# Delta rule: values scaled by the key norm in the input projection, written by an identity product into the bank of the error sum, and copied by ScalarE

## The chip, the cores and the metric

The kernel runs on one core of a Trainium2 chip. The metric is the device time of one execution in microseconds (us); lower is better. A profile is one execution recorded by the hardware profiler, whose times count from the start of its span. The engines are named as in the profile: PE is TensorE's matmul, PEld its weight load, DVE is VectorE, ACT is ScalarE, POOL is GpSimd, and SP is the queue from which most transfers (DMAs) are issued. PSUM is the memory that PE writes, in eight banks. Lines of the kernel are written L613.

## The reference, cut to what matters

A two-layer encoder step over 2048 prompt tokens and 32 sample tokens. The first layer is a gated delta rule with 8 heads of 128 channels; the change lies there.

```
proj = x @ w_in                                   # q, k, v rows, then the gate z
qkv  = silu(causal_conv(proj_qkv))                # four taps per channel
q = l2norm(q) / sqrt(128);  k = l2norm(k)
S_t = exp(g_t) (I - beta_t k_t k_t^T) S_{t-1} + beta_t k_t v_t^T
o_t = S_t^T q_t                                   # evaluated exactly, in chunks
```

In a chunk, the error of the values is `v - (k * exp(gcum)) S`: what the new values hold beyond what the state S already predicts. A triangular inverse turns the errors into the changes of the state. The kernel does not normalize k in advance. It works with the raw k, which is the normalized k times its norm, and so needs the values times that norm: `v * hn - (k_raw * exp(gcum)) S`, with hn the key's norm for each token and head.

## The kernel before, in words

**Input projection (up to about 610 us).** `P1.qkv` runs 24 rows, each one head's 128 channels of q (rows 0 to 7), k (8 to 15) or v (16 to 23) over all 2080 tokens. A row is five blocks of 416 tokens, each with 24 matmuls into one PSUM bank (L77 to L79). The banks of these blocks are six: two in pool `ppl`, four in pool `ppr`. ACT copies each block into the row's buffer `R` (L309), of which there are two, so row i + 2 needs the buffer of row i. Then come the four taps (L293 on ACT, three times L295 on DVE) into `y` (two buffers), a tanh on ACT (L275), the product that makes the silu (L276, DVE), and the store of y to DRAM (L278 on SP; a small remainder on ACT's queue). q and k rows also give sums of squares. After row 15 `norms` computes hn (L456) from them, with a power on POOL (L468). Beside this, `presplit` splits weights of later stages (L95, L96) and stores them (L97). Here the order on every engine and queue is chosen by the framework's planner, which simulates a timeline as it places instructions. It is fixed before the run.

**Between the stages (about 610 to 745 us).** The rows' memory is given up (`mid.close()`), and its place is taken by tiles whose loads (L512, L514, L529, L532) SP issues. PE goes on with the gate z, whose blocks are finished by L321 on ACT and L322, L323 on DVE and stored at L324. Two chunks' triangular inverses are computed ahead by DVE.

**Delta loop (`Delta.run`, about 745 to 1165 us).** There are 17 chunks: chunk 0 is the 32 sample tokens, chunks 1 to 16 are 128 prompt tokens each. Iteration i finishes chunk i (`ch`), and prepares chunks i + 1 (`nx`), i + 2 (`n2`) and i + 3 (`n3`). On PE, DVE and ACT the instructions run in exactly the order in which `run` steps through generators (`go`), each step being one `yield`. The names that matter:

- `lower` (L562, L563, L567, L570, L572): products of keys, and the matrix L for the triangular chain.
- `chain` (L585, L588): the triangular inverse, its first 25 of 31 steps on POOL, the rest (t in `run`) on DVE.
- `spread` (L653, L654): transposes of the inverse, tcp; `invert` (L672 to L708): the larger inverse out of the blocks. L672 on PE needs tcp, and L674 on ACT, which writes y1, needs L672.
- `turn_v` (L612, L613): per half of four heads, four transposes of v into a bank of the pair "tr", then one DVE instruction that multiplies by hn into the tile vn.
- `errors` (L717, L718): per half, four products k S into a bank of the pair "sc", then one DVE subtraction from vn.
- `changes` (L728, L730): the inverse times vn; `seen` (L742, L746, L750): the output, two products into one bank, copied by ACT; `squares` (L776) and `powers` (L636) on ACT; `advance` (L760, L766): the new state S; `inside` (L627, L628): q k products gq, into a bank of "tr"; `fade` (L644): k and q times exp(gcum); `emit` (L802, L803): output transposed, times z.
- `fill`: in iterations 0 to 10 it hands PE pieces of the rest of the z projection (L77 to L79, 6 matmuls a piece) at fixed places.

In an iteration the order around the change is: advance, seen, squares of the first half; the second half of seen; squares; `powers(n2)`; a filler; errors, t, spread; turn_v, errors; inside; a filler; invert and the rest.

Of the kernel before, what the change touches and what calls it, by code (L numbers as in the profile page):

```python
# [10 lines left out]
F32 = mybir.dt.float32  # L11
# [3 lines left out]
ALU = mybir.AluOpType  # L15
# [5 lines left out]
NP = 2048  # L21
NS = 32
NT = NP + NS
# [3 lines left out]
H = 8  # L27
# [4 lines left out]
NTT = 17  # L32
# [130 lines left out]
class P1:  # L163
# [49 lines left out]
    def qkv(self):  # L213
        nc, I, T, G, big, one = self.nc, self.I, self.T, self.G, self.big, self.one
# [11 lines left out]
        for b in range(NB):  # L226
            ps = self.ps()
            xh, xl = self.x[b]
            for k in range(KC):
                nc.tensor.matmul(ps[:48, :TB], wab[:, k, :48], xh[:, k, :], start=(k == 0), stop=False,  # L230
                                 skip_group_check=True)
# [3 lines left out]
            for t in range(b * TB // 128, NTT if b == NB - 1 else (b + 1) * TB // 128):  # L235
                n = min(128, NT - t * 128)
# [13 lines left out]
        for i in range(24):  # L250
            kind, h = i // 8, i % 8
            if i < 2:
                R = Rs[i]
            else:
                w = split_weights(nc, self.wp, I["w_in"][i], nc.gpsimd)
                R = self.row(i)
                if i == 23:
                    gate = self.split_gate(nc.gpsimd)
                    first = next(gate)
                for b in range(NB):  # L260
                    self.block(R, w, b)
# [12 lines left out]
            th = one.tile([128, NT + 3], F32, tag="th", name="th")  # L274
            nc.scalar.activation(th[:], y[:], AF.Tanh, scale=0.5)  # L275
            nc.vector.scalar_tensor_tensor(out=y[:], in0=th[:], scalar=1.0, in1=y[:], op0=ALU.add, op1=ALU.mult)  # L276
            dst = T["qkv"[kind]]
            nc.sync.dma_start(dst[0:NTT - 1, :, h, :].rearrange("t p k -> p t k"),  # L278
                              y[:, 0:NP].rearrange("p (t k) -> p t k", k=128))
            nc.scalar.dma_start(dst[NTT - 1, :, h, 0:NS], y[:, NP + 3:NP + 3 + NS])  # L280
            if kind == 2:
                continue
            nc.scalar.activation(th[:, 0:NP], y[:, 0:NP], AF.Square)
            nc.scalar.activation(th[:, NP:NT], y[:, NP + 3:NP + 3 + NS], AF.Square)
            nc.vector.transpose(R[:, 0:NT], th[:, 0:NT])
            nc.vector.tensor_reduce(out=parts[:, h, :], in_=R[:, 0:NT].rearrange("p (c j) -> p c j", j=32),
                                    axis=AX.X, op=ALU.add)
            if h == 7:
                norms(nc, G, parts, self.sel, kind, one, self.pt)
        nc.sync.dma_start(self.O["conv"][:, :, :], self.convo[:])  # L290

    def conv(self, y, R, i, a, z):
        self.nc.scalar.activation(y[:, a:z], R[:, a:z], AF.Copy, scale=self.convw[:, i, 0:1])  # L293
# [146 lines left out]
def norms(nc, G, parts, sel, kind, one, pt):  # L440
    V = nc.vector
    ps = pt.tile([128, 512], F32, tag="tp", name="n_ps")
    pv = ps[:, 0:H * NTT].rearrange("p (h t) -> p h t", h=H)
    for c in range(4):
        m = NTT if c == 0 else NTT - 1
        nc.tensor.matmul(pv[:, :, 0:m], sel[:, c, :], parts[:, :, c::4], start=(c == 0), stop=(c == 3))
    w = H * NTT
    x = one.tile([128, w], F32, tag="n_x", name="n_x")
    V.tensor_scalar(out=x[:].rearrange("p (t h) -> p t h", h=H), in0=pv.rearrange("p h t -> p t h"),
                    scalar1=4e-6, scalar2=None, op0=ALU.add)  # L450
    xv = x[:].rearrange("p (t h) -> p t h", h=H)
    if kind == 0:
        V.tensor_scalar(out=G["eq"][:], in0=xv, scalar1=128.0 * RMS_EPS, scalar2=None, op0=ALU.mult)
        return
    rv = rsqrt_power(nc, G, one, x[:], 128, w, "n")[:].rearrange("p (t h) -> p t h", h=H)
    V.scalar_tensor_tensor(out=G["hn"][:], in0=xv, scalar=0.5, in1=rv, op0=ALU.mult, op1=ALU.mult)  # L456
# [20 lines left out]
class Delta:  # L477
# [124 lines left out]
            ch.kd.append(kd)  # L602
            yield

    def turn_v(self, ch):
        nc, G, n = self.nc, self.G, ch.n
        ch.vn = []
        for q in range(2):
            vn = self.four.tile([128, 4, 128], F32, tag="vn", name="vn")
            tr = self.pa.tile([128, 4, 128], F32, tag="tr", name="vtr")  # L610
            for j in range(4):
                nc.tensor.transpose(tr[:n, j, :], ch.v[q][:, j, :n], G["ident"][:, :])  # L612
            nc.vector.tensor_tensor(out=vn[:n], in0=tr[:n], in1=self.bc(G["hn"][:n, ch.ti, q * 4:q * 4 + 4], n),  # L613
                                    op=ALU.mult)
            ch.vn.append(vn)
            yield

    def inside(self, ch):

        nc, V, n = self.nc, self.nc.vector, ch.n  # L620
# [18 lines left out]
    def fade(self, ch):  # L639

        n = ch.n
        for x in (ch.k, ch.q):
            for q in range(2):
                self.nc.vector.tensor_tensor(out=x[q][:, :, :n], in0=x[q][:, :, :n], in1=ch.gb[q][:, :, :n], op=ALU.mult)  # L644
                yield

    def spread(self, ch):
# [62 lines left out]

    def errors(self, ch):

        nc, V, n = self.nc, self.nc.vector, ch.n
        for q in range(2):
            ks = self.pc.tile([128, 4, 128], F32, tag="sc", name="ks")
            for j in range(4):
                nc.tensor.matmul(ks[:n, j, :], ch.k[q][:, j, :n], self.S[q][:, j, :], start=True, stop=True)  # L717
            V.tensor_tensor(out=ch.vn[q][:n], in0=ch.vn[q][:n], in1=ks[:n], op=ALU.subtract)  # L718
            yield

    def changes(self, ch):
# [85 lines left out]
    def run(self, chunks, S, first, second, side, done):  # L807
# [7 lines left out]
        def go(*gens):  # L815
            for g in gens:
                next(g, None)

        c0, c1, c2 = chunks[:3]
        for c in (c0, c1):  # L820
            for name in ("gb", "k", "q"):
                self.load(c, name)
            if c is c0:
                self.load(c, "v")
# [6 lines left out]
        k, w, g, d, low = self.turn_k(c0), self.turn_v(c0), self.inside(c0), self.decays(c1), self.lower(c1)  # L831
        for s, us in ((w, 0.6), (k, 0.6), (w, 0.6), (k, 0.6), (g, 0.6), (g, 0.6), (d, 0.0), (d, 0.0), (d, 1.2), (d, 1.2),
                      (low, 1.2), (low, 1.2)):
            go(s)
            fill(us)
        drain(self.powers(c0))
        drain(self.fade(c0))
        self.load(c1, "v")
        self.load(c2, "gb")
        self.spread(c0)  # L840
        k, w, g = self.turn_k(c1), self.turn_v(c1), self.inside(c1)
        for s, us in ((k, 1.0), (w, 1.0), (k, 1.0), (w, 1.0), (g, 1.0), (g, 1.0)):
# [6 lines left out]
        go(e, e, seen)  # L849
        self.load(c2, "k")  # L850
        self.load(c2, "q")
        last, z, x = None, none, self.fade(c1)
# [1 line left out]
        for i in range(len(chunks) + 1):  # L854
# [7 lines left out]
                                                   (lambda c: self.chain(c, V, self.SPLIT, 31), nx)))  # L862
            low = gen(self.lower, n2)
            go(low, x, low)
            if n2:
                self.load(n2, "v", (0,))
# [8 lines left out]
            fill(2 * more)  # L875
            go(seen, a, t, a, t)
            fill(more)
            go(sq, seen)
            if n2:
                self.load(n2, "v", (1,))  # L880
            if n3:
                self.load(n3, "q", (0,))
            side()
# [13 lines left out]
            if i == 0:  # L897
                self.save("s_delta")
                self.S = S
            k, w, g, e, v, r, o = (gen(f, c) for f, c in (  # L900
                (self.turn_k, n2), (self.turn_v, n2), (self.inside, n2), (self.errors, nx), (self.invert, nx),
                (self.norms, ch), (self.scale, ch)))
            go(e, t, t)
            drain(t)
            if nx:
                self.spread(nx)
            go(w, e)
            if n3:
                self.load(n3, "k")
            go(g)  # L910
# [1 line left out]
            d = gen(self.decays, n3)  # L912
            go(v, r, r, r, g, r, r, v, r, k, r, d)
            side()
            go(v, w, r, d)
            if i:
                self.load(ch, "z")
            fill(more)
            seen = gen(self.seen, nx)
            go(r, r, seen, v, k, d, r, r)  # L920
            if n3:
# [1 line left out]
            fill(more)  # L923
            drain(r)
            go(o)
            side()
            if i in (13, 14):
                second.step()
# [1091 lines left out]
def host_inputs(inp):  # L2020
# [56 lines left out]
    "v": (NTT, 128, 8, 128),  # L2077
    "z": (8, 128, NT),
    "gcum": (NTT, 8, 128),
    "o": (NS, 8, 128),  # L2080
    "g": (NTT, 128, 8, 128),
    "h": (NT, D),
# [50 lines left out]
```

## Time and profile before

| | |
|---|---|
| time, median of 3 runs | 2183.53 us (2180.78 to 2184.08) |
| the profiled execution's own time | 2181.37 us |
| its span, first to last instruction | 2179.6 us |
| mean granted TensorE clock | 0.986 |
| instructions | 37384 |
| PE busy over the span | 2068.7 us, 95% |
| DVE, ACT, POOL busy | 1477.4, 906.8, 725.1 us |

Busy time is a sum over stages that have different limits, so it is read by stage. A timeline row gives start, length, engine, line, what is written from what, and in brackets how long the engine had stood and for whom. The iterations of the delta loop are told apart by tcp (L653), which runs once in each: iteration 0 at 760.15 us, 2 at 809.27, 6 at 913.53, 9 at 990.04, 13 at 1088.23. An fp32 product on PE shows as two records, a transpose as one.

### The profile page before, as it was taken

How to read it: one execution, taken by the hardware profiler on the slowest of the kernel's cores; microseconds unless marked ns; L12 is line 12 of the kernel's file. 1: busy time of each engine (PE TensorE's matmuls, PEld its weight loads, DVE VectorE, ACT ScalarE, POOL GpSimd, SP SyncE). 2: the span in 40 equal slices, each digit the busy share in tenths (PEclk: the TensorE clock that was granted, in tenths of full speed). 3: DMA queues.
4: the chain of work that ended last, by engine and by line, in shares of the span. 5: the costliest groups of instructions: out<-in, count | busy, mean ns of one | idle time of the engine just before them, and what ended most of it. 6: DMA issues, size and time to landing. Idle time of an engine off the chain costs nothing. (4 is left out here: it accounts for less than half of the span.)

```text
span 2179.6 us, 37384 instructions
## 1 busy us (share of the span) xinstructions
PE 2068.7 (95%) x13494; PEld 1874.1 (86%) x13494; DVE 1477.4 (68%) x2767; ACT 906.8 (42%) x2405; POOL 725.1 (33%) x1194
## 2 busy tenths in 40 slices
PE   8999999999989999999789999999999988999998
PEld 6999999999989889888778887899999976777666
DVE  5788977886557588888875665555645655666663
ACT  5545545444422476767662111411221033444441
POOL 1212211151111187878861220000000053666565
PEclk9999999999999999999999999999999999999999
DMA  7755655557764644534845675988888885433321
GB/s 283 226 187 192 214 180 185 188 180 244 257 211 157 209 128 153 163 130 152 274 144 148 209 264 192 340 290 278 291 279 282 283 291 168 110 85 93 99 81 58
DMA packets 342410, 430.28 MB, mean 197 GB/s; under 512 B 69952, under 2 KB 269984, under 8 KB 342208
## 3 DMA queue, kind: packets, MB, share of 16 engines
q1 hardware_dynamic: 304016, 304.78, 44.0%
q10 hardware_dynamic: 38208, 123.10, 16.9%
q8 instruction: 107, 1.75, 0.3%
q14 instruction: 79, 0.65, 0.1%
HBM read 269.72 MB, written 158.44 MB: 196 GB/s over the span
## 5 line engine op out<-in xcount | busy, mean ns | idle before, releaser
L77 PE MATMUL ps<-act_hi,w_hi 128*128 128x416 f32 x1280 | 458.6, 358 | 5.7 <-DVE z L322 2.5
L79 PE MATMUL ps<-act_hi,w_lo 128*128 128x416 f32 x1280 | 450.5, 353 | 4.7 <-POOL w_lo L54 3.3
L78 PE MATMUL ps<-act_lo,w_hi 128*128 128x416 f32 x1280 | 451.1, 352 | 0.0
L77 PEld LDWEIGHTS ps<-act_hi,w_hi 128*128 128x128 f32 x1280 | 242.0, 189 | 10.1 <-DVE z L322 4.3
L79 PEld LDWEIGHTS ps<-act_hi,w_lo 128*128 128x128 f32 x1280 | 241.9, 189 | 9.5 <-POOL w_lo L54 4.4
L78 PEld LDWEIGHTS ps<-act_lo,w_hi 128*128 128x128 f32 x1280 | 242.6, 190 | 2.8
L1330 PE MATMUL ps<-xs_h,w 128*128 128x416 f32 x560 | 199.6, 356 | 7.8 <-DVE ra L1391 6.6
L1331 PE MATMUL ps<-xs_l,w 128*128 128x416 f32 x560 | 199.9, 357 | 0.5 <-DVE xs_l L1228 0.5
L54 POOL TENSOR_TENSOR w_lo<-w_raw,w_hi 128x1024 fp32r<-128x1024 f32 x32 | 81.5, 2547 | 355.2 <-ACT w_hi L53 341.2
L1332 PE MATMUL ps<-xs_h,w 128*128 128x416 f32 x560 | 198.6, 355 | 0.0
L295 DVE SCALAR_TENSOR_TENSOR y<-R,convw,y 128x2083 f32<-128x2083 f32 (+2 forms) x78 | 175.1, 2245 | 24.5 <-ACT y L293 24.3
L1615 ACT ACTIVATE P<-S,nm 128x192 f32<-128x192 f32 (+2 forms) x260 | 105.3, 428 | 177.4 <-DVE nm L1604 170.8
L585 POOL TENSOR_TENSOR tm<-L,Tt 128x60 f32<-128x60 f32 (+19 forms) x375 | 136.3, 363 | 94.2 <-PE sp L760 48.9
L588 POOL TENSOR_TENSOR Tt<-Tt,tm 128x60 f32<-128x60 f32 (+19 forms) x375 | 142.0, 379 | 28.3
L1530 POOL MEMSET vd<- 64x768 f32 (+2 forms) x10 | 7.8, 776 | 398.1 <-DVE ra L1391 397.8
L1627 POOL TENSOR_TENSOR P<-P,sm 128x512 f32<-128x512 f32 (+2 forms) x126 | 101.7, 831 | 87.8 <-DVE sm L1624 69.2
L1330 PEld LDWEIGHTS ps<-xs_h,w 128*128 128x128 f32 x560 | 106.5, 190 | 10.6 <-DVE ra L1391 7.3
L1391 DVE SCALAR_TENSOR_TENSOR ra<-ps,u 128x416 f32<-128x416 f32 x60 | 35.4, 590 | 117.3 <-PE ps L1332 110.7
L1052 PE MATMUL po<-wo,g_hi 128*128 128x512 f32 (+1 forms) x272 | 110.0, 404 | 0.9 <-DVE hT L1100 0.9
L1332 PEld LDWEIGHTS ps<-xs_h,w 128*128 128x128 f32 x560 | 107.1, 191 | 1.3
L1331 PEld LDWEIGHTS ps<-xs_l,w 128*128 128x128 f32 x560 | 106.3, 190 | 2.1 <-DVE xs_l L1228 0.7
L95 ACT CAST pre_hl<-pre_raw 128x256 fp32r<-128x256 f32 x184 | 65.6, 404 | 101.4 <-DMA pre_raw<-in_b_w_z 25.8
(313 smaller groups left out, 4723.6 us busy)
## 6 DMA issues: line engine op xcount, KB each, us to landing
w<-s_w ACTq DMA_DIRECT2D x180, 512.0 KB, 4.5
s_w<-pre_hl SPq DMA_DIRECT2D x160, 256.0 KB, 2.5
w_raw<-in_w_in SPq DMA_DIRECT2D x32, 512.0 KB, 6.6
s_wo<-pre_hl SPq DMA_DIRECT2D x64, 256.0 KB, 4.1
gb<-s_gcum SPq DMA_DIRECT2D x34, 256.0 KB, 5.2
k<-s_k SPq DMA_DIRECT2D x34, 256.0 KB, 3.8
s_z<-z SPq DMA_DIRECT2D x40, 208.0 KB, 2.0
s_q<-y SPq DMA_DIRECT2D x8, 1024.0 KB, 5.2
```

The lines of the kernel that those rows point to most:

```text
L77: nc.tensor.matmul(ps, hi[:, k, :], xh[:, k, :], start=(k == 0), stop=False)
L78: nc.tensor.matmul(ps, hi[:, k, :], xl[:, k, :], start=False, stop=False)
L79: nc.tensor.matmul(ps, lo[:, k, :], xh[:, k, :], start=False, stop=(k == KC - 1))
L295: self.nc.vector.scalar_tensor_tensor(out=y[:, a:z], in0=R[:, a + j:z + j], scalar=self.convw[:, i, j:j + 1], in1=y[:, a:z], op0=ALU.mult, ...
L585: P.tensor_tensor(out=tm[:n, i0 - k:, :w], in0=L[:n, i0:, j:j + 1].to_broadcast(sh), in1=Tt[:n, j:j + 1, :w].to_broadcast(sh), op=ALU.mult)
L588: P.tensor_tensor(out=Tt[:n, i0:, :w], in0=Tt[:n, i0:, :w], in1=tm[:n, i0 - k:, :w], op=ALU.subtract)
L1052: nc.tensor.matmul(ps[:n], ghi[:, k, :n], w[0][k][:, cs], start=(k == 0), stop=False)
L1330: nc.tensor.matmul(ps, w[:, 0, k], xh[:], start=first and k == 0, stop=False, skip_group_check=True)
L1331: nc.tensor.matmul(ps, w[:, 0, k], xl[:], start=False, stop=False, skip_group_check=True)
L1332: nc.tensor.matmul(ps, w[:, 1, k], xh[:], start=False, stop=last and k == 3, skip_group_check=True)
L1615: nc.scalar.activation(P[:, u, :nk], S[:, u, :], AF.Exp, bias=nm[:, u:u + 1], scale=1.0, accum_out=sm[:, u:u + 1])
L1627: nc.gpsimd.tensor_tensor(out=out, in0=part, in1=f, op=ALU.mult)
```

## The change

The values are multiplied by hn as soon as they leave the silu, in channel-major form. For that, `key_norms` transposes hn after row 15, and writes it to a new DRAM array `hnr` (chunk, head, token). Each v row then loads its head's part, repeated over the 128 partitions, into its own R buffer, from ACT's queue, and DVE multiplies y by it before the store.

In the delta loop `turn_v` is gone. `errors` has four steps instead of two: in the first two, four products v^T x identity open a bank of "tr" for each half; in the last two, four products k S go into the same bank on top, and ACT copies the bank to vn. `fade` negates k by the way, so that the sum is the difference. The first two steps stand ahead of the squares and of the second half of seen; the loads of v move to the end of the iteration; the steps of the opening get the same filler in other portions.

```
             nc.vector.scalar_tensor_tensor(out=y[:], in0=th[:], scalar=1.0, in1=y[:], op0=ALU.add, op1=ALU.mult)
+            if kind == 2:
+                nc.scalar.dma_start(R[:, 0:NP].rearrange("p (t k) -> p t k", k=128),
+                                    T["hnr"][0:NTT - 1, h, :].partition_broadcast(128))
+                nc.scalar.dma_start(R[:, NP + 3:NP + 3 + NS], T["hnr"][NTT - 1, h, 0:NS].partition_broadcast(128))
+                nc.vector.tensor_tensor(out=y[:], in0=y[:], in1=R[:, 0:NT + 3], op=ALU.mult)
...
+                if kind == 1:
+                    self.key_norms()
...
+    def key_norms(self):
+        nc, hn = self.nc, self.G["hn"]
+        for t0, w, n in ((0, NTT - 1, 128), (NTT - 1, 1, NS)):
+            tp = self.pt.tile([128, 512], F32, tag="tp", name="tp")
+            nc.tensor.transpose(tp[:w * H, :n], hn[:n, t0:t0 + w, :].rearrange("p t h -> p (t h)"), self.G["ident"][:n, :n])
+            rows = self.one.tile([128, 128], F32, tag="g_row", name="rows", bufs=2)
+            nc.vector.tensor_copy(rows[:w * H, :n], tp[:w * H, :n])
+            nc.sync.dma_start(self.T["hnr"][t0:t0 + w, :, :n].rearrange("t h k -> (t h) k"), rows[:w * H, :n])
...
     def fade(self, ch):
-        for x in (ch.k, ch.q):
+        for x, sign in ((ch.k, -1.0), (ch.q, 1.0)):
-                self.nc.vector.tensor_tensor(out=x[q][:, :, :n], in0=x[q][:, :, :n], in1=ch.gb[q][:, :, :n], op=ALU.mult)
+                self.nc.vector.scalar_tensor_tensor(out=x[q][:, :, :n], in0=x[q][:, :, :n], scalar=sign,
+                                                    in1=ch.gb[q][:, :, :n], op0=ALU.mult, op1=ALU.mult)
...
     def errors(self, ch):
+        ch.vn, banks = [], []
         for q in range(2):
-            ks = self.pc.tile([128, 4, 128], F32, tag="sc", name="ks")
+            ks = self.pa.tile([128, 4, 128], F32, tag="tr", name="ks")
             for j in range(4):
-                nc.tensor.matmul(ks[:n, j, :], ch.k[q][:, j, :n], self.S[q][:, j, :], start=True, stop=True)
-            V.tensor_tensor(out=ch.vn[q][:n], in0=ch.vn[q][:n], in1=ks[:n], op=ALU.subtract)
+                nc.tensor.matmul(ks[:n, j, :], ch.v[q][:, j, :n], self.G["ident"][:, :], start=(j == 0), stop=False,
+                                 skip_group_check=True)
+            banks.append(ks)
+            yield
+        for q in range(2):
+            for j in range(4):
+                nc.tensor.matmul(banks[q][:n, j, :], ch.k[q][:, j, :n], self.S[q][:, j, :], start=False, stop=(j == 3),
+                                 skip_group_check=True)
+            vn = self.four.tile([128, 4, 128], F32, tag="vn", name="vn")
+            nc.scalar.copy(vn[:n], banks[q][:n])
+            ch.vn.append(vn)
             yield
...
-            go(sq, seen)
-            if n2:
-                self.load(n2, "v", (1,))
+            go(e, e, sq, seen)
...
             go(e, t, t)
             drain(t)
             if nx:
                 self.spread(nx)
-            go(w, e)
+            go(e)
```

More of the change, by code (lines that the diff above doesn't have):

```diff
@@ L603, in turn_k @@
             yield
[L605 to L616, printed above, removed]
     def inside(self, ch):
@@ L711, in errors @@
     def errors(self, ch):
-        nc, V, n = self.nc, self.nc.vector, ch.n
+        nc, n = self.nc, ch.n
+        ch.vn, banks = [], []
         for q in range(2):
-            ks = self.pc.tile([128, 4, 128], F32, tag="sc", name="ks")
+            ks = self.pa.tile([128, 4, 128], F32, tag="tr", name="ks")
             for j in range(4):
-                nc.tensor.matmul(ks[:n, j, :], ch.k[q][:, j, :n], self.S[q][:, j, :], start=True, stop=True)
-            V.tensor_tensor(out=ch.vn[q][:n], in0=ch.vn[q][:n], in1=ks[:n], op=ALU.subtract)
+                nc.tensor.matmul(ks[:n, j, :], ch.v[q][:, j, :n], self.G["ident"][:, :], start=(j == 0), stop=False,
[9 more added lines that the diff above has]
+            ch.vn.append(vn)
             yield
@@ L822, in run @@
                 self.load(c, name)
-            if c is c0:
-                self.load(c, "v")
+        self.load(c0, "v")
+        self.load(c1, "v")
         fill = first.give
@@ L830, in run @@
         fill(1.0)
-        k, w, g, d, low = self.turn_k(c0), self.turn_v(c0), self.inside(c0), self.decays(c1), self.lower(c1)
-        for s, us in ((w, 0.6), (k, 0.6), (w, 0.6), (k, 0.6), (g, 0.6), (g, 0.6), (d, 0.0), (d, 0.0), (d, 1.2), (d, 1.2),
+        k, g, d, low = self.turn_k(c0), self.inside(c0), self.decays(c1), self.lower(c1)
+        for s, us in ((k, 1.2), (k, 1.2), (g, 0.6), (g, 0.6), (d, 0.0), (d, 0.0), (d, 1.2), (d, 1.2),
                       (low, 1.2), (low, 1.2)):
@@ L837, in run @@
         drain(self.fade(c0))
-        self.load(c1, "v")
         self.load(c2, "gb")
         self.spread(c0)
-        k, w, g = self.turn_k(c1), self.turn_v(c1), self.inside(c1)
-        for s, us in ((k, 1.0), (w, 1.0), (k, 1.0), (w, 1.0), (g, 1.0), (g, 1.0)):
+        k, g = self.turn_k(c1), self.inside(c1)
+        for s, us in ((k, 1.5), (k, 1.5), (g, 1.5), (g, 1.5)):
             go(s)
@@ L848, in run @@
         e, seen = self.errors(c0), self.seen(c0)
-        go(e, e, seen)
+        go(e, e, e, e, seen)
         self.load(c2, "k")
@@ L864, in run @@
             go(low, x, low)
-            if n2:
-                self.load(n2, "v", (0,))
+            e = gen(self.errors, nx)
             go(vp, vp, z, z, x, x, low, low, t)
@@ L877, in run @@
             fill(more)
-            go(sq, seen)
-            if n2:
-                self.load(n2, "v", (1,))
+            go(e, e, sq, seen)
             if n3:
@@ L899, in run @@
                 self.S = S
-            k, w, g, e, v, r, o = (gen(f, c) for f, c in (
-                (self.turn_k, n2), (self.turn_v, n2), (self.inside, n2), (self.errors, nx), (self.invert, nx),
-                (self.norms, ch), (self.scale, ch)))
+            k, g, v, r, o = (gen(f, c) for f, c in (
+                (self.turn_k, n2), (self.inside, n2), (self.invert, nx), (self.norms, ch), (self.scale, ch)))
             go(e, t, t)
@@ L914, in run @@
             side()
-            go(v, w, r, d)
+            go(v, r, d)
             if i:
@@ L918, in run @@
             fill(more)
+            if n2:
+                self.load(n2, "v", (0,))
             seen = gen(self.seen, nx)
@@ L925, in run @@
             go(o)
+            if n2:
+                self.load(n2, "v", (1,))
             side()
@@ L2079 @@
     "gcum": (NTT, 8, 128),
+    "hnr": (NTT, 8, 128),
     "o": (NS, 8, 128),
```

## The prediction, made before the changed kernel was run

> **What bounds the kernel now.** I read the page's first part, then busy time by stage, then the waits of the delta loop, then the loop's timeline engine by engine.
>
> ```profile
> PE 2068.7 (95%) x13494; PEld 1874.1 (86%) x13494; DVE 1477.4 (68%) x2767; ACT 906.8 (42%) x2405; POOL 725.1 (33%) x1194
> 460.00:500.00 40.00, 40.00 (x214) 39.61 (x213) 30.23 (x46) 17.82 (x32) 15.98 (x14) 1.00 0.61 198
> 620.00:640.00 20.00, 15.01 (x72) 13.37 (x73) 11.28 (x19) 6.23 (x18) 2.35 (x1) 0.83 0.68 246
> 913.53:939.25 25.72, 23.86 (x273) 21.90 (x273) 21.47 (x49) 17.65 (x57) 20.40 (x52) 1.00 0.56 175
> 1064.58:1088.23 23.65, 19.27 (x248) 17.66 (x248) 21.30 (x47) 17.14 (x56) 19.82 (x51) 1.00 0.70 218
> ```
>
> The stage rows give start and end, length, then busy time of PE, PEld, DVE, ACT and POOL, the granted clock, the DMA share and GB/s. In the input projection (460 to 500) PE never pauses: what is added beside it is free while PE keeps running, and every pause of PE is paid in full. The delta loop (one chunk per row from 913 on) has no full engine: DVE 21.5 and PE 23.9 of 25.7 us. There a hand-written order, not a sum of work, makes the period.
>
> ```profile
> POOL tm L585 <- DVE tm L585: 16.7, 9, 4.3
> ```
>
> Between 745 and 1130 POOL, which runs the triangular chain, waits only 16.7 us, 9 times. The change does not touch that chain, so the loop can at best lose those 16.7 us, whatever DVE is spared.
>
> **The delta loop.** Per chunk it removes two transposes' copies (L613) and two subtractions (L718) from DVE and puts two copies on ACT.
>
> ```profile
> L718 DVE TENSOR_TENSOR vn<-vn,ks 128x512 f32<-128x512 f32 (+1 forms) x34 | 22.9, 674 | 7.8 <-PE ks L717 7.6
> L613 DVE TENSOR_TENSOR vn<-vtr,t_hn 128x512 f32<-128x512 f32 (+1 forms) x34 | 22.9, 672 | 7.3 <-PE vtr L612 6.8
> L730 ACT COPY vs<-vp 128x512 f32<-128x512 f32 (+1 forms) x34 | 19.7, 587 | 15.4 <-PE vp L728 15.2
> ```
>
> DVE loses 2 x 0.674 + 2 x 0.672 = 2.7 us per chunk; ACT gains 2 x 0.59 = 1.2 us, priced by L730, a copy of the same shape out of the same kind of bank. What of it lies on the path? One chunk (iteration 6):
>
> ```profile
> 909.88 0.58 ACT L750 COPY o<-op 128x512 f32<-128x512 f32 x1 [1.76 <-PE op L746]
> 909.95 1.16 PE L717 MATMUL ks<-Sp,k 128*128 128x128 f32 x8
> 910.94 0.60 PE L612 MATMUL vtr<-ident,v 128*128 128x128 f32 x4
> 911.16 0.68 DVE L718 TENSOR_TENSOR vn<-vn,ks 128x512 f32<-128x512 f32 x1
> 911.38 1.06 PE L717 MATMUL ks<-Sp,k 128*128 128x128 f32 x8
> 911.69 1.13 ACT L636 ACTIVATE gb<-gb 128x512 f32<-128x512 f32 x2
> 912.27 1.06 PE L627 MATMUL gq<-q,k 128*128 128x128 f32 x8
> 913.53 0.72 DVE L653 STREAM_TRANSPOSE tcp<-Tt 128x256 f32<-128x256 f32 x1
> 914.39 0.69 PE L672 MATMUL bps<-tcp,npr 32*32 32x32 f32 x32
> 915.13 0.76 ACT L674 ACTIVATE y<-bps 32x256 f32<-32x256 f32 x2 [2.31 <-PE bps L672]
> 915.36 1.16 PE L627 MATMUL gq<-q,k 128*128 128x128 f32 x8 [0.28 <-DVE vn L613]
> 924.74 0.65 DVE L322 TENSOR_SCALAR z<-ps,nwh 128x416 f32<-128x416 f32 x1 [3.46 <-ACT zth L321]
> ```
>
> From ACT's y (915.13) ACT is the late engine for 9 us, until DVE, at 924.74, is kept waiting by it; from there DVE runs to tcp (913.53, one chunk earlier), then PE starts L672 and ACT its y. Of the four removed DVE instructions only the first L718 (911.16) stands ahead of tcp: tcp comes 0.6 us earlier. The other three stand where DVE waits for ACT anyway; the one visible return is that the second gq no longer waits 0.28 us for L613.
>
> PE pays. Four transposes take 911.38 - 910.94 = 0.44 us, four fp32 products (eight passes) 912.27 - 911.38 = 0.89 us. The eight identity products cost 1.78 us, against 0.88 for the eight transposes, and all of them now stand ahead of the two halves of seen (L742, L746). ACT's copy of seen was waiting for just that PE work (909.88, 1.76 us idle), so it comes 1.78 us later, and with it, in ACT's order, four squares and the two exponentials of L636. Only behind L636 comes the new copy of the first bank. Both error banks are now of the "tr" pair that gq (L627) also takes, so gq waits for that copy. In iteration 6: L636 ends at 911.69 + 1.13 + 1.78 = 914.60, the copy at 915.19; gq starts 915.2 instead of 912.27, and L672, with the filler between, 2.9 us later than 914.39. Less the 0.28 returned, ACT's y and all behind it come 2.6 us later. ACT's idle 2.31 us would have hidden the 1.2 us of copies, but not copies that start 1.8 us late with PE waiting behind them.
>
> ```profile
> 806.67 1.13 ACT L636 ACTIVATE gb<-gb 128x512 f32<-128x512 f32 x2
> 808.01 1.06 PE L627 MATMUL gq<-q,k 128*128 128x128 f32 x8
> 810.00 0.69 PE L672 MATMUL bps<-tcp,npr 32*32 32x32 f32 x32 [0.93 <-DVE tcp L653]
> 985.50 0.59 ACT L750 COPY o<-op 128x512 f32<-128x512 f32 x1 [0.83 <-PE op L746]
> 987.30 1.13 ACT L636 ACTIVATE gb<-gb 128x512 f32<-128x512 f32 x2
> 988.79 1.06 PE L627 MATMUL gq<-q,k 128*128 128x128 f32 x8
> 1084.78 1.13 ACT L636 ACTIVATE gb<-gb 128x512 f32<-128x512 f32 x2
> 1088.95 0.69 PE L672 MATMUL bps<-tcp,npr 32*32 32x32 f32 x32 [1.12 <-DVE tcp L653]
> ```
>
> The same step elsewhere. Iteration 2 (fillers ahead of ks): copy done at 806.67 + 1.13 + 1.78 + 0.59 = 810.17, gq 0.89 behind it, so L672 at 811.1 instead of 810.0: 1.1, less 0.3, is 0.8. Iteration 9: copy done 990.8 against gq at 988.79: 2.0 - 0.3 = 1.7. Iteration 13 (no filler): copy done 1088.28, L672 at 1089.2 instead of 1088.95: 0.2, and there POOL's chain sets the period, so nothing. By the iteration that each resembles: 0 to 3 at 0.8, 4 to 6 at 2.6, 7 to 10 at 1.7, 11 and 15 at 0.8, 12 to 14 nothing: 3.2 + 7.8 + 6.8 + 1.6 = 19.4 us. Bounds: none of it, if the path from y back to seen has slack that I don't see; 26, if iterations 11 to 15 pay like 7. Below nothing, the first L718 gives 0.6 in 11 chunks, -7. I take 19.
>
> At nothing: the fade as scalar_tensor_tensor is still one pass over two SBUF tensors. The v loads stay 34 and move to SP's later slots, over 10 us before use. Ahead of the loop, four groups of transposes (1.76 us) leave and two of products (1.78) come.
>
> **The input projection.** Each of the last 8 rows gets a 1 MB broadcast into its R buffer and a DVE multiply (2.33 us, priced by L276 below, same shape). Beside a saturated PE that is hidden, except in the first such row.
>
> ```profile
> 438.36 0.10 POOL L300 MEMSET R<- 128x3 f32 x1 [2.73 <-DVE y L295]
> 442.08 24.09 POOL L468 TENSOR_TENSOR n_y<-n_x,half 128x136 f32<-128x136 f32 x1 [3.48 <-DVE n_x L449]
> 450.57 0.51 ACT L309 COPY R<-ps 128x416 f32<-128x416 f32 x1 [1.06 <-PE ps L79]
> 466.20 2.50 DVE L456 SCALAR_TENSOR_TENSOR t_hn<-n_x,n_y 128x136 f32<-128x136 f32 x1 [2.52 <-POOL n_y L468]
> 468.66 0.57 ACT L309 COPY R<-ps 128x384 f32<-128x384 f32 x2 [4.03 <-PE ps L79]
> s_v<-y SPq DMA_DIRECT2D x8, 1024.0 KB, 5.6
> s_z<-z SPq DMA_DIRECT2D x40, 208.0 KB, 2.0
> ```
>
> The key norms need a power on POOL that takes 24 us; hn is finished at 466.20 + 2.50 = 468.7. Row 16's R buffer is free at 438.36 now, after its last conv step; in the change it is kept until row 16's multiply. Row 18 needs that buffer; its first block is evicted at 450.57, its fifth leaves PE at 468.66. There are six PSUM banks (ppl 2, ppr 4). One block is 24 matmuls at 40 / 214 = 0.187 us, 4.5 us; so the sixth bank is full at 473.1. The buffer comes free at: 468.7 + 0.6 (transposes, as L612) + 0.7 (row copy, as L718) + 2.4 (write: 2.0 landing, 0.4 issue) + 6.0 (1 MB: 5.6 and 0.4) + 2.3 (multiply) + 0.5 (first eviction) = 481.2. PE stands 8.1 us: from 5, if hn is not stretched as now, to 16, if the row copy queues behind a conv step and the broadcast lands late.
>
> When PE has stood, the granted clock falls: 0.83 over 620 to 640, with 5.0 us of PE idle, is 3.4 us lost in clock. After one stop I count 1.9, between nothing and that 3.4. The Trainium skill ("TensorE: Matmul & The Clock Gate", Part 1) says that an idle window of about 3.4 us halves the clock and that it takes as long of work to restore it; by that rule the loss is about 1.7 us and the total 0.2 lower. First row: 10.
>
> ```profile
> 599.67 2.33 DVE L276 SCALAR_TENSOR_TENSOR y<-th,y 128x2083 f32<-128x2083 f32 x1 [2.01 <-ACT th L275]
> 607.64 0.62 SPq L512 DMA_DIRECT2D nm<-in_nm  x1
> 614.10 0.45 SPq L324 DMA_DIRECT2D s_z<-z  x1
> 620.61 0.65 DVE L322 TENSOR_SCALAR z<-ps,nwh 128x416 f32<-128x416 f32 x1 [14.89 <-DMA s_z<-z]
> ```
>
> At the end the last row's y is stored a multiply and part of a broadcast later: 2.3 us up to 2.3 + 6.0. The next stage's loads (607.64) take over that memory, the store of z (614.10) stands behind them on SP, and DVE's z waits for it, with PE soon behind. Between nothing, if the planner puts that store ahead, and 8, I take 4.
>
> **Sum.** 19 + 10 + 4 = 33 us on the profiled execution's 2181.4 (span 2179.6), so 2214.4. The median of the runs is 2.2 above that execution: 2216.6. Own range: 0 + 5 + 0 to 26 + 19 + 8, most likely 2193 to 2232.
>
> **Rivals.** *Vector relief* (faster): DVE at 21.5 of 25.7 is the nearest thing to a bound, and the copies fit into ACT's 2.31 idle us. It decides where L636 does not move, that is, where the identity products find PE idle: then tcp gains 0.6 in 11 chunks, and if the first row's buffer comes free before 473.1, the time is 2183.5 - 6.6 = 2177; POOL's waits allow at most 2183.5 - 16.7 = 2167. Against it: ACT's copy of seen waits for PE in both quoted chunks (1.76 and 0.83 us). *Washed out* (same): relief and the two stops cancel, 2183. *Power blocks PE*: the new transposes sit in PE's queue before hn is ready; PE then stands from near 445 to 469, 24 us, and the banks never fill: 14 more than forecast, 2231. For it: that order is fixed ahead of time; against: DVE's hn waited only 2.5 us for the power, so the planner knows its length. That the change doesn't do what it says, I see no room for: seen already adds two products in one bank.
>
> **Chances.** Forecast 0.77, vector relief 0.11, washed out 0.05, power blocks PE 0.07. A difference under 0.2% (4.4 us) cannot be told from none here. Slower 0.84, same 0.05, faster 0.11. The range reaches to 2186 below, which leaves out relief, wash and little more, and to 2234 above, past the power case.
>
> **What would show it.** Right: a PE gap of 5 to 16 us near 473 with row 18's first eviction near 481; gq in iterations 4 to 10 waiting for ACT's vn copy; periods of 27 to 28 us there, 23.65 still in 13 and 14. Wrong: L636 where it was, periods under 25.7, PE unbroken from 460 to 500.

## The result, and the profile after

The changed kernel takes 2294.57 us (median of 4, 2292.76 to 2300.89) against 2182.16 for the kernel before: a ratio of 1.0514, with a 95% interval of 1.0497 to 1.0531. That is 112 us slower where 33 were forecast. The profiled execution spans 2292.2 us. The first row of its page:

```profile
PE 2096.2 (91%) x13632; PEld 1899.0 (83%) x13632; DVE 1462.7 (64%) x2709; ACT 922.6 (40%) x2439; POOL 721.5 (31%) x1194
```

The rows by stage, in the same columns as in the prediction:

```profile
460.00:500.00 40.00, 13.42 (x71) 12.65 (x69) 19.58 (x41) 5.29 (x11) 12.06 (x7) 0.73 0.49 149
500.00:540.00 40.00, 33.47 (x163) 32.95 (x164) 20.04 (x23) 15.23 (x28) 3.48 (x7) 0.85 0.64 173
580.00:620.00 40.00, 31.40 (x143) 29.57 (x142) 20.95 (x23) 12.91 (x22) 3.25 (x5) 0.87 0.82 197
640.00:680.00 40.00, 19.10 (x80) 17.27 (x81) 16.42 (x14) 11.71 (x18) 4.69 (x6) 0.67 0.72 204
984.02:1012.49 28.47, 24.87 (x282) 22.98 (x280) 19.63 (x45) 18.76 (x61) 18.96 (x51) 1.00 0.39 123
```

TensorE, unbroken before from 460 to 500, now works 13.4 us of those 40. From 506.5 to 586 it runs on without a stop, then it stops five more times, for 3.7 to 18.6 us, and the granted clock over 40 us falls to 0.67. To divide the 112.6 us between the two profiled executions I use the start of tcp, once per chunk. The first comes at 829.1 us instead of 734.8: 94.4 us in the input projection. From the first to the seventeenth it takes 417.0 us instead of 403.4: 13.6 in the loop. From there to the end 1046.1 instead of 1041.5: 4.6.

The first stop, by the timelines of VectorE, ScalarE's queue and TensorE:

```profile
466.03 2.50 DVE L473 SCALAR_TENSOR_TENSOR t_hn<-n_x,n_y 128x136 f32<-128x136 f32 x1 [2.32 <-POOL n_y L485]
471.58 0.37 DVE L306 COPY rows<-tp 128x128 f32<-128x128 f32 x2
474.62 5.28 ACTq L280 DMA_DIRECT2D R<-s_hnr  x1
482.61 11.11 ACTq L280 DMA_DIRECT2D R<-s_hnr  x1
494.25 0.43 DVE L96 TENSOR_TENSOR pre_hl<-s,pre_hl 128x256 fp32r<-128x256 f32 x1 [15.49 <-ACT pre_hl L95]
495.35 2.32 DVE L281 TENSOR_TENSOR y<-y,R 128x2083 f32<-128x2083 f32 x1
505.97 2.21 ACT L326 COPY R<-ps 128x416 f32<-128x416 f32 x6 [11.45 <-DMA pre_raw<-in_b_w_z]
506.53 0.71 PE L77 MATMUL ps<-act_hi,w_hi 128*128 128x416 f32 x1 [33.11 <-ACT R L326]
```

hn is finished at 468.5, as forecast (468.7), and the norm rows are ready at 472. Then the forecast's chain breaks: the multiply runs at 495.35, not at 478.4, and the first eviction only at 505.97, not at 481.2. ACT's queue first issues the second row's broadcasts (11.11 us for the small one). A cast of ACT stands behind them, and VectorE waits 15.49 us for that cast ahead of its multiply. ACT then waits for weights to split (pre_raw) that stand ahead of the evictions in its order.

The price behind it is in the list of DMA issues (count, KB each, median us to landing); that it is the cause is tested below:

```profile
R<-s_hnr ACTq DMA_DIRECT2D x8, 1024.0 KB, 16.4
```

The broadcast of 1 MB takes 16.4 us where the prediction put 6.0, the price of a 1 MB store.

In the loop, the end of the period of 28.47 us in the rows by stage (25.77 before) shows the forecast chain (timelines of ScalarE and TensorE):

```profile
1010.73 0.58 ACT L765 COPY o<-op 128x512 f32<-128x512 f32 x1 [3.53 <-PE op L761]
1012.53 1.13 ACT L640 ACTIVATE gb<-gb 128x512 f32<-128x512 f32 x2
1013.57 1.04 ACT L732 COPY vn<-ks 128x512 f32<-128x512 f32 x2
1014.18 1.16 PE L631 MATMUL gq<-q,k 128*128 128x128 f32 x8 [1.71 <-ACT vn L732]
```

ACT's copy of seen waits 3.53 us for TensorE, where it waited 1.76. The exponentials follow it, then the new copies, and gq waits 1.71 us for the first copy. The list of waits from the first to the last tcp (829 to 1246 us; us, times, longest) has the sum:

```profile
PE gq L631 <- ACT vn L732: 16.3, 15, 1.7
```

### The profile page after: what moved, and what is told of

The parts are those of the page before. It is cut to its first block, busy times and chain, and to the rows that moved or that the text cites. A ratio compares the mean times of both kernels' runs of the same rounds, so it can differ in the third digit from the quotient of the medians.

```text
span 2292.2 us, 37665 instructions
## 1 busy us (share of the span) xinstructions
PE 2096.2 (91%) x13632; PEld 1899.0 (83%) x13632; DVE 1462.7 (64%) x2709; ACT 922.6 (40%) x2439; POOL 721.5 (31%) x1194
## 5 line engine op out<-in xcount | busy, mean ns | idle before, releaser
L79 PE MATMUL ps<-act_hi,w_lo 128*128 128x416 f32 x1280 | 455.8, 357 | 6.9 <-POOL w_lo L54 5.9
L79 PEld LDWEIGHTS ps<-act_hi,w_lo 128*128 128x128 f32 x1280 | 244.4, 191 | 13.4 <-POOL w_lo L54 8.5
L602 POOL TENSOR_TENSOR tm<-L,Tt 128x60 f32<-128x60 f32 (+19 forms) x375 | 129.1, 344 | 113.6 <-PE sp L775 49.7
```

Of the source, the lines that this page charges most:

```text
L79: nc.tensor.matmul(ps, lo[:, k, :], xh[:, k, :], start=False, stop=(k == KC - 1))
L602: P.tensor_tensor(out=tm[:n, i0 - k:, :w], in0=L[:n, i0:, j:j + 1].to_broadcast(sh), in1=Tt[:n, j:j + 1, :w].to_broadcast(sh), op=ALU.mult)
```

## The experiments

First come the parts. **e1_loop** keeps the changed loop alone (values not scaled by the key norm), **e2_input** the input projection's part alone (values scaled twice).

```
e1_loop:  - if kind == 2: the two broadcasts, the multiply;  - self.key_norms()   (from the changed kernel)
e2_input: + the same lines                                                        (to the kernel before)
```

> The delta loop's part alone: the changed loop, with the input projection as it was before. It leaves out the scaling of the values by the key norm. In the changed kernel's profile the first tcp of the loop comes 94.4 us later than before, the sixteen periods of the loop take 12.8 us more and the stretch from the last tcp to the end 4.6 us more. Theory (the two parts add up, and the loop's costs are its own): 2182.2 + 0.8 + 12.8 + 4.6 = 2200, between 2194 and 2204. Rival (the loop's loss is a consequence of the late input projection, for instance through loads and stores that meet differently): within 5 us of 2182. Rival (the prediction's loop sum of 19 was right and the longer input projection hid some of it): 2201 to 2206.

> The input projection's part alone: the norm rows, the broadcasts and the multiply of the changed kernel, with the loop of before. The values are scaled by the key norm twice. Theory (the parts add up): 2182.2 + 94.4 = 2276.6, between 2268 and 2283. Rival (a part of the 94 us is made by what the loop's change does to the planner's order or to the start of the loop): below 2262.

Measured: e1_loop 2197.77 us against 2182.62, ratio 1.0074 (1.0059 to 1.009), so 15.2 us. e2_input 2276.48, 1.0442 (1.0423 to 1.0461), so 93.9 us. Together 109 of 112: the parts add up. The loop's own loss is smaller than the forecast's 19; the input projection's is 80 us larger than its 14 (10 for the first row, 4 for the end).

**e3_dense** stores the norm rows by head, so that a partition of the broadcast reads one run of 8 KB. **e4_nobc** drops the broadcasts and multiplies by what R still holds (no scaling by the key norm).

```
e3_dense: "hnr": (8, NP);  dma_start(R[:, 0:NP], T["hnr"][h, :].partition_broadcast(128))
e4_nobc:  - nc.scalar.dma_start(R[...], T["hnr"]...)    (both)
```

> The changed kernel, but the scratch copy of the norm rows lies by head, so that each partition of a broadcast reads one run of 8 KB instead of 16 runs of 512 bytes 4 KB apart. Theory A (the broadcast is slow because it is cut into 512-byte pieces: 16.4 us to landing against 5.6 for a 1 MB store): it lands in 5 to 7 us, the rows after the first cost nothing, and about 10 to 25 of the 94 us remain: 2211 to 2226. Rival B (the order of the queues stops the evictions whatever the broadcast takes, since ACT's queue issues it and the store behind it): the stops shorten by about 10 us a row only where the broadcast ends the wait, 2235 to 2265. Rival C (a megabyte read from one place costs 16 us in any layout, because of what else the queues carry at that time): 2288 to 2300.

> The changed kernel without the two broadcasts of each value row: the multiply stays and takes the row's own R buffer as its second factor, so the values are not scaled by the key norm; the power, the transposes and the store of the norm rows stay. Theory (all of the input projection's loss is waiting for the broadcast): 2182.2 + 18.2 for the loop and the tail = 2200, between 2194 and 2208, with no stop of TensorE over 3 us between 460 and 720 us. Rival (the 2.33 us multiply in VectorE's order, or the key norms' own steps, already delay the conv steps and through them the evictions): 2215 or more.

Measured: e3_dense 2215.41, ratio 1.0157 (1.0141 to 1.0172); e4_nobc 2196.83, 1.0072 (1.0048 to 1.0096). The broadcast among the DMA issues of e3_dense:

```profile
R<-s_hnr ACTq DMA_DIRECT2D x8, 1024.0 KB, 6.4
```

TensorE's longest waits there in the input projection (us, times, longest):

```profile
PE ps L77 <- ACT R L328: 12.5, 1, 12.5
PE ps L77 <- ACT w_hi L53: 3.9, 2, 3.0
```

The same megabyte lands in 6.4 us, and only the first row's stop, 12.5 us, is left of any size. Theory A holds: the layout in 512-byte pieces, 4 KB apart, makes the slow broadcast (no run tells the size of the pieces from their distance), and the slow broadcast costs 79 us. Without a broadcast (e4_nobc) the time is that of the loop's part alone, so the multiply, the transposes and the norm store cost nothing that can be told.

**Which path leads from the broadcast to TensorE?** My first theory was ACT's queue: it issues the broadcasts, and the small store behind the multiply stands ahead of the evictions. e9_store moves that store to SP's queue, e10_sync the broadcasts as well.

```
- nc.scalar.dma_start(dst[NTT - 1, :, h, 0:NS], ...)
+ (nc.sync if kind == 2 else nc.scalar).dma_start(dst[NTT - 1, :, h, 0:NS], ...)
- nc.scalar.dma_start(R[...], T["hnr"]...)      (e10_sync only, both)
+ nc.sync.dma_start(R[...], T["hnr"]...)
```

> The changed kernel with one edit: the small store of each value row's last 32 tokens, which waits for the multiply, is issued on SP's queue instead of ACT's. The slow broadcast (16.4 us) stays. Theory (most of the 94 us is ACT's queue standing at that store with the evictions and the weight casts behind it): the stops of the last rows shrink, 30 to 70 of the 94 us return: 2225 to 2265. Rival (VectorE's in-order wait for the broadcast and the R buffer behind it are enough to stop TensorE): 2280 to 2297. Second rival (ACT's queue at that store was all): under 2215.

> As e9_store, and the two broadcasts of each value row on SP's queue too, so that ACT's queue issues nothing for the scaling. The broadcast is still cut into 512-byte pieces. Theory (the time of the broadcast itself reaches TensorE over VectorE's order, R and SP's queue, where the weight loads now stand behind it): within 15 us of e9_store, on either side. Rival (the issue on ACT's queue, up to 11 us in the trace of the changed kernel, was the larger part): 25 us or more below e9_store.

Measured: 2293.23, ratio 1.0496 (1.0473 to 1.052), and 2289.96, 1.0484 (1.0455 to 1.0513). That theory falls: 1 and 5 us came back. The second was a ring through VectorE's order, in which the multiply stands ahead of the next row's conv steps. e12_order puts it behind the next row's silu (in short, not the lines themselves):

```
+ hold = y * 0 + 1                       # one column of the next row's y, on VectorE
- y = y * R
+ y_previous = y_previous * hold * R_previous, then its stores
```

> The changed kernel with its slow broadcast (512-byte pieces, issued on ACT's queue) and its stores in place. One edit: the multiply of a value row stands behind the next row's conv steps and silu in VectorE's order, held there by a factor of one made from that row's values. e9_store and e10_sync, 2293.2 and 2290.0 us against 2294.6, have set aside the theory that ACT's queue makes the stops. New theory (a ring through VectorE's order: broadcast 16.4, multiply 2.3, the next row's three conv steps 7.2, tanh 2.0, silu 2.3, then the next broadcast, 30 us a row against 22.5 us of TensorE's work): with the multiply behind the next silu the ring is cut, the rows after the first cost nothing, and the first row's stop, with the multiply at about 489 us instead of 478, is 19 us and 4 of clock: 2182.6 + 15.2 + 23 = 2221, between 2210 and 2240. Rival (the R buffer or the queues carry the broadcast's time to TensorE in any order): 2265 or more.

Measured: 2305.63, ratio 1.0544 (1.0523 to 1.0565). This edit decides nothing: it adds a wait of its own (ACT's first conv step waits 22.6 us, 6 times, for the store of an older y), and the weights for the split still come late (39.6 us of ACT waiting for them). So each path was taken away by itself. e13_free multiplies by the tanh's buffer, so VectorE waits for no broadcast (no scaling by the key norm). e14_nosplit keeps that wait and ends the weight splitting with row 15 (the later stages read other split weights). e15_both does both.

```
e13_free:    - in1=R[:, 0:NT + 3]                     + in1=th[:]
e14_nosplit: - due += 224 / 20 if i >= 4 else 0       + due += 224 / 20 if 4 <= i < 16 else 0
             - while due >= 1 or i == 23:             + while due >= 1:
```

> The changed kernel with its slow broadcasts in place, each still held in R, but the multiply takes the tanh's buffer as its second factor, so that VectorE waits for no broadcast. The values are not scaled by the key norm. Ring theory (VectorE's order: broadcast, multiply, the next row's conv steps, tanh, silu, then the next broadcast, 30 us a row): only the first row's stop is left, 30 to 40 us with the clock: 2182.6 + 15.2 + 35 = 2233, between 2220 and 2245. Rival (while a broadcast runs, the trace of the changed kernel shows the 16 DMA engines up to 1.00 busy at 72 to 94 GB/s, against 264 to 411 before; the weights for the split, which ACT casts in its order ahead of the evictions, land late, and that stops TensorE without VectorE's wait): 2270 or more.

> The changed kernel with its slow broadcasts and the waiting multiply, but with the side work of the value rows left out: the splitting of the later stages' weights (loads, ACT's casts, VectorE's subtractions, stores) ends with row 15, and the later stages read other split weights in place of the missing ones, so their values are not the reference's. Ring theory (VectorE waits for the broadcast in its order): the rows still take about 30 us, 2270 or more. Rival (the late loads and the casts behind them on ACT carry the broadcast's time to TensorE): only the first row's stop is left, 20 to 35 us: 2182.6 + 15.2 + 28 = 2226, between 2212 and 2240.

> e13_free and e14_nosplit in one kernel: the slow broadcasts run and are held in R, but VectorE does not wait for them (the multiply takes the tanh's buffer, so the values are not scaled by the key norm), and the weight splitting of the value rows is left out, with other split weights read in its place. Alone the two left 61 and 73 us of the 94 in the stretch up to the first tcp. Theory (two paths side by side, VectorE's ring of 30 us a row and the late loads whose casts stand in ACT's order, each enough to stop TensorE): with both cut only the first row's stop is left, 20 to 35 us: 2182.6 + 15.2 + 28 = 2226, between 2214 and 2238. Rival (a third path, R held until the broadcast lands or ACT's own issue of it, still gives rows of 30 us): 2250 or more.

Measured: e13_free 2275.49 us, ratio 1.0425 (1.0403 to 1.0446); e14_nosplit 2264.01, 1.0373 (1.0353 to 1.0394); e15_both 2218.95, 1.0168 (1.0145 to 1.0191). Neither theory alone: there are two paths side by side, and each is enough. The first tcp comes 73.2, 60.9 and 18.5 us later than in the kernel before, against 94.4 in the changed kernel: only with both cut does the time fall to the loop's part and one stop (13.3 us, the first row's). The ring, in e14_nosplit's VectorE timeline:

```profile
564.86 2.33 DVE L276 SCALAR_TENSOR_TENSOR y<-th,y 128x2083 f32<-128x2083 f32 x1 [2.02 <-ACT th L275]
578.53 2.33 DVE L281 TENSOR_TENSOR y<-y,R 128x2083 f32<-128x2083 f32 x1 [11.34 <-DMA R<-s_hnr]
585.04 7.24 DVE L312 SCALAR_TENSOR_TENSOR y<-R,convw,y 128x2083 f32<-128x2083 f32 x3 [4.18 <-ACT y L310]
594.29 2.33 DVE L276 SCALAR_TENSOR_TENSOR y<-th,y 128x2083 f32<-128x2083 f32 x1 [2.01 <-ACT th L275]
```

From silu to silu: 2.33 + 11.34 (rest of the broadcast) + 2.33 + 4.18 + 7.24 + 2.01 = 29.43 us, just the distance from 564.86 to 594.29. The 4.18 us are ACT's: its small store waits for the multiply, and the next cast, two evictions and the first tap stand behind it. A row of TensorE is 5 blocks of 4.5 us, 22.5. With a broadcast that lands 10 us earlier the ring is 19.4 and stays inside 22.5; that is why e3_dense pays nothing there.

The other path is the weights that ACT splits: they land late. In these stage rows of 4 us the last two columns are the DMA engines' share and GB/s. The changed kernel, while a broadcast runs:

```profile
560.00:564.00 4.00, 4.00 (x23) 3.97 (x22) 1.43 (x4) 3.92 (x9) 1.47 (x1) 1.00 0.75 68
592.00:596.00 4.00, 4.00 (x17) 3.87 (x17) 0.00 (x0) 0.00 (x0) 0.00 (x0) 0.71 0.89 72
```

The kernel before, in the first of the two:

```profile
560.00:564.00 4.00, 4.00 (x23) 3.96 (x22) 1.36 (x1) 2.52 (x4) 2.67 (x3) 1.00 0.99 322
```

The DMA engines are 0.75 to 0.89 busy and move 68 to 72 GB/s; before, 0.99 moved 322, 3.6 to 4 times as much for the share. What else wants them waits. In e13_free, in which VectorE is free, a load of 512 KB that falls beside the broadcasts (in_b_w_out) takes 10.7 us to landing, one of the same size in the first 200 us (in_a_w_out) 4.0:

```profile
pre_raw<-in_a_w_out SPq DMA_DIRECT2D x8, 512.0 KB, 4.0
pre_raw<-in_b_w_out SPq DMA_DIRECT2D x8, 512.0 KB, 10.7
```

Its waits from 500 to 720 us:

```profile
ACT pre_hl L95 <- DMA pre_raw<-in_b_w_out: 44.0, 6, 12.8
PE ps L77 <- ACT w_hi L53: 21.9, 3, 15.5
PE ps L77 <- ACT R L326: 13.0, 2, 8.4
```

ACT's casts wait for the weights, and the evictions and the next row's cast stand behind them in ACT's order. In the kernel before, the same loads held ACT 24.3 us in 5 waits of at most 6.6, and no stop of TensorE there was over 2.5 us. That the loads are late because the broadcast holds the engines is read from these rows; no run here changes the engines' share alone, and e14_nosplit takes away the whole splitting, not the late loads alone.

**The first row, and the loop's order.** e7_keysfirst is e3_dense with the key rows projected before the query rows, so that hn is ready long before row 16. e5_afterseen is the loop's part alone with the identity products behind both halves of seen; e6_dve the loop's part with VectorE making the new copies. (Both leave out the scaling by the key norm.)

```
e7_keysfirst: - for i in range(24):        + for pos, i in enumerate([*range(8, 16), *range(8), *range(16, 24)]):
e5_afterseen: - go(e, e, sq, seen)         + go(sq, seen)
              - go(a, t, a, t, seen, sq)   + go(a, t, a, t, seen, sq, e, e)
e6_dve:       - nc.scalar.copy(vn[:n], banks[q][:n])   + nc.vector.tensor_copy(vn[:n], banks[q][:n])
```

> e3_dense (2215.4 us, norm rows laid by head) with the key rows projected first, then the query rows, then the value rows: the key norms are finished about 150 us before the first value row needs them. Theory (what is left of the input projection's loss in e3_dense, 14.7 us up to the first tcp, is the first row's wait for the norm): 2215.4 - 14.7 = 2200.7, between 2196 and 2206, with no stop of TensorE over 3 us between 460 and 600 us. Rival (it is the longer chain of each value row, or the buffer R held for the multiply): 2209 or more.

> The loop's part alone (as in e1_loop: no scaling of the values by the key norm), with one move: the identity products of both error banks stand behind both halves of seen in TensorE's order instead of ahead of the second. e1_loop took 2197.8 us; against before its periods 1, 2 and 5 to 11 are longer by 2.6, 0.45, 2.1, 2.7, 2.0, 1.55, 1.5, 1.7 and 1.5 us. Theory (the loss is the 1.78 us of identity products ahead of ACT's copy of seen, which put the exponentials, the new copies and gq later): ACT comes 1.78 us earlier, each of those periods gets back its loss up to 1.8 us, 13.9 in all: 2184, between 2180 and 2189. Rival (the bank is what costs: gq waits for copies that stand behind the exponentials wherever the identity products are): 2193 to 2198.

> The loop's part alone (as in e1_loop), with the copies of the error banks on VectorE instead of ScalarE, in the place in the order where the subtractions were; the identity products stay ahead of seen. In the changed kernel's period that starts at 1012.49, the second error bank is ready at about 1012.3, ScalarE's copies run only at 1013.57 behind the exponentials, and gq starts at 1014.18. Theory (late exponentials and the copies behind them): a VectorE copy ends at about 1013.0, gq starts 1.2 us earlier, and about 1 us of each of periods 5 to 11 comes back, less 0.67 ahead of tcp where tcp is late: 2191, between 2187 and 2195. Rival (the copy waits on VectorE ahead of the last steps of the chain and tcp, and the loss stays): 2196 or more.

Measured: e7_keysfirst 2205.86, ratio 1.0102 (1.0087 to 1.0117). The first tcp is at 736.1 us, 13.5 earlier than in e3_dense, and no stop between 440 and 600 is over 1.2 us: the first row's wait for the norm is shown. Its total is at the upper end of what was expected, because its loop came out 5.8 us longer than e3_dense's with the same order (periods 0, 12 and 15); that stays unexplained. e5_afterseen 2189.22, 1.0025 (1.0012 to 1.0038): 8.6 us less than e1_loop, where 13.9 were expected, and just past the upper end of the expected 2180 to 2189. Each of its periods 5 to 11 is 0.5 to 2.0 us shorter than e1_loop's, but period 1 is 31.54 us instead of 27.09, at a lower clock (0.88; last section), and the last chunk's y comes 6.6 us after tcp. In the profile of e11_filler (below), whose loop has the same order at that place, the clock is 1.00 and period 1 is 27.37 us, so most of that period's excess is the clock. So the place of the identity products makes a good part of the loop's loss, and the rival, the bank wherever they stand, does not make it alone. e6_dve 2206.36, 1.0103 (1.0088 to 1.0118): 8.6 us slower than e1_loop, a miss. The rival that was named is what happened: VectorE waits for the error sum (19.1 us, 14 times) ahead of the chain's last steps, and TensorE then waits for tcp (8.0 us, 7 times; in e1_loop not at all).

**e8_all** joins the three mends and keeps the whole computation; **e11_filler** also moves the last chunk's filler matmuls behind the first step of its inversion.

> All three mended together, the whole computation kept: norm rows by head, key rows first, identity products behind both halves of seen. Theory: e7_keysfirst's 2200.7 less the 13.9 of the loop, 2187, between 2181 and 2193, so about the kernel before. Rival (one of the mends fails or they are not independent): 2197 or more.

> e8_all (2187.6 us; the whole computation) with one more edit for the last chunk alone: the filler matmuls that stood between the second half of seen, the error sums and the last inversion are given behind the inversion's first step. In e5_afterseen y of the last chunk comes 6.6 us after tcp, before 2.2 us. Theory (that is the filler ahead of the error sum): 4 us less, 2183.5, between 2180 and 2186, not to be told from the kernel before. Rival (the fillers are needed there and stand in the way later): 2187 or more.

Measured: e8_all 2187.61, ratio 1.0025 (1.0006 to 1.0044); e11_filler 2187.77, 1.0024 (1.0008 to 1.004). The three mends return 107 of the 112 us. The filler's move shows in the profiled execution (1044.3 us from the last tcp to the end, against 1047.6), but not in the medians, so its gain is not shown. No version here beats the kernel before; with all three mends the change still comes out 0.25% slower (0.06 to 0.44).

## Why the prediction was wrong

The direction, the loop's mechanism and the place of the first stop were right. But 80 of the 112 us come from the value rows, which the prediction put at nothing beyond the first: one price was wrong and, with it, one sentence. Point by point:

- **Delta loop, 19 (0 to 26): right in its mechanism, the total in part by luck.** Measured 15.2 alone. Number the periods from tcp to tcp from 0; a chunk's delay shows in the period after its tcp. Where 2.6 was forecast for three (iterations 4 to 6, periods 5 to 7) the changed kernel is longer by 2.05, 2.70 and 1.92; where 1.7 was forecast for four (periods 8 to 11) by 1.62, 1.55, 1.58 and 1.56. gq waits for ACT's copy, as written. These seven periods make 13.0 us of the 14.6 forecast. The rest came out near only because its errors cancel, as the next two points show.
- **Where the loop's forecast missed.** Period 1 got 2.6 us longer, where 0.8 was forecast; why is not known. Periods 3 and 4 got shorter, by 2.7 and 1.3 us. Before, they ran at a lowered clock (third last column), in the changed kernel at 1.00; the prediction took each period of before as it stood and never asked for its clock. The kernel before, then the changed one:

```profile
809.27:837.07 27.80, 26.17 (x272) 24.68 (x272) 22.04 (x50) 17.78 (x57) 19.69 (x51) 0.88 0.50 159
837.07:863.44 26.37, 25.05 (x268) 23.66 (x269) 22.28 (x49) 17.79 (x57) 18.56 (x48) 0.87 0.42 126
```

```profile
907.39:932.53 25.14, 24.38 (x283) 23.10 (x281) 19.78 (x46) 18.62 (x61) 20.15 (x52) 1.00 0.55 176
932.53:957.65 25.12, 24.36 (x287) 23.07 (x285) 19.80 (x46) 18.60 (x61) 20.12 (x52) 1.00 0.35 109
```

- **The tail.** From the last tcp on, it costs 4.6 us (5.5 in e1_loop), not 0.8. In e1_loop the last chunk's y comes 5.3 us after tcp instead of 2.2, behind the error sum and the fillers.
- **First value row, 10: half right.** hn's end, the buffer R as the link and the place of the stop were right. The size was not: a stop of 33.1 us instead of 8.1, since behind R there also stood ACT's queue and the late weights. With the broadcast at 6.4 us (e3_dense) the stop is 12.5, inside the forecast's 5 to 16.
- **The broadcast at 6.0: the step that failed.** It was priced by a store of the same bytes (5.6). The store writes from 128 partitions; the broadcast reads 16 runs of 512 bytes for each of 128 partitions. It measured 16.4.
- **"Beside a saturated PE that is hidden, except in the first such row": failed with it.** I compared engine time with TensorE's time, and never added the chain of one row. With 6.4 the sentence holds (e3_dense: 2215.4 us, where 2216.6 was forecast; the two are so near in part because the first stop, 12.5 us instead of 8.1, makes up for the end, near nothing instead of 4); with 16.4 the ring is 29.4 us against 22.5, and a second path through the loads is as long. The range had no room for this since no rival priced the broadcast otherwise.
- **End of the phase, 4: too much.** Once the broadcast is short, the first tcp is within 1.6 us of e1_loop's (736.1 against 734.5, e7_keysfirst).
- **Rivals.** Power blocks PE: no; the transposes run at 468.68 and TensorE works until the banks are full. Vector relief: no; VectorE's busy time in the quoted period fell to 19.63 of 28.47 us and the period grew.

On the clock: the Trainium skill ("TensorE: Matmul & The Clock Gate", Part 1) has an idle window of about 3.4 us halve the clock. The long stop agrees: after 33.1 us of standing the granted clock is 0.50 from 506.5 to 512 us and 0.95 over the next 4 us.

## What to carry to other kernels

Price a DMA by its pieces, not by its bytes: look for a row with the same run length and the same direction, and if there is none, let the range reach to several times the bulk price. For work that is "hidden" beside a full engine, add up one whole round of it in the order of the engines that carry it, waits included, and compare that with the full engine's round; it is hidden up to that point and paid in full past it. When one cut brings nothing back, a second path of the same length may be standing behind it: cut both at once before giving up a theory.

## What the runs showed of the hardware

- A 1 MB broadcast of one DRAM row to 128 partitions: 16.4 us in 512-byte runs 4 KB apart, 6.4 us in 8 KB runs. While the first runs, the DMA engines are 0.75 and 0.89 busy in the two rows above, at 68 and 72 GB/s. The Trainium skill ("DMA: Bandwidth & Descriptors", "Why small descriptors are slow (HBM only)") names a fixed cost of about 3 cycles a packet beside one cycle for 32 bytes, and 32 bytes of descriptor for each operation; for 512 bytes that makes 19 cycles for 16 and 6% more, an estimate of 1.26 x 6.4 = 8.1 us. The run says 16.4, so what else makes short runs slow here stays open.
- The DMA issued right behind such a broadcast occupies the queue: the 16 KB remainders of the first two rows took 5.28 and 11.11 us to issue (rows above) and those of the other six 3.10 to 5.74, against 0.44 to 0.65 us behind a broadcast in 8 KB runs (e3_dense).
- The clock can fall without a long stop. In e5_afterseen TensorE's last wait before is 1.44 us, at 746 us, and ten us later, with TensorE busy all the time, the rows read:

```profile
745.00:750.00 5.00, 3.56 (x32) 3.20 (x30) 1.01 (x2) 0.76 (x2) 0.00 (x0) 1.00 0.70 218
750.00:755.00 5.00, 5.00 (x39) 4.25 (x37) 3.20 (x5) 3.77 (x10) 0.00 (x0) 1.00 0.31 106
755.00:760.00 5.00, 5.00 (x26) 3.55 (x25) 4.22 (x11) 1.13 (x9) 3.13 (x12) 0.56 0.35 91
760.00:765.00 5.00, 5.00 (x21) 4.93 (x22) 0.00 (x0) 2.83 (x11) 3.98 (x14) 0.50 0.45 128
```

No idle window of 3.4 us stands ahead of it, so the rule quoted above does not explain this one; before, and in e1_loop, the clock in these rows is 1.00 with waits of about the same length (1.21 and 1.38 us). The profile of e8_all has such a dip too (0.53 from 760 to 765), that of e11_filler, with the same order at that place, has none. What sets it off stays open.
